# A decoder layer on one core: the output product's results kept in fixed PSUM banks, its operands formed three steps ahead by GpSimd

## The chip, the core and the metric

The kernel runs on one core of a Trainium2 chip. The core has five engines that run side by side, each with its own queue, in order: TensorE (PE in the profile; PEld are its weight loads), VectorE (DVE), ScalarE (ACT), GpSimd (POOL) and SyncE (SP), which here only issues transfers. TensorE writes its products into PSUM, eight banks of 128 x 512 float32; VectorE and ScalarE read and write PSUM and SBUF, GpSimd and transfers SBUF alone. The metric is the device time of one execution in microseconds (us).

## The reference, cut to what matters

One layer, 1024 tokens by 1024 columns, float32. Only the end of it is touched:

```python
y_conv = (u * silu(z_conv)) @ w_conv_out
y_att = (att * silu(z_att)) @ w_att_out
merged = sigmoid(g_conv) * y_conv + sigmoid(g_att) * y_att
x = x + gate * (merged @ w_o)
return x * rsqrt(mean(x * x) + EPS) * final_g
```

## The kernel before

**Split products.** Every float32 operand is split in a high half (a ScalarE copy to a rounded type) and a low half (value minus high half, on VectorE or GpSimd). `mm3` (lines 72 to 75) multiplies high by high (line 73), high by low and low by high, so one 128 x 128 block costs three products. A step of the last stages is 12 products of 128 x 512.

**Steps.** The code calls `at(step, rank, fn)` to put a piece of work at a step. `serve_steps` (line 1064) then goes through the steps and writes the instructions out: first EARLY, then the step's group of products, then COPY, EVICT and HIGH (ScalarE), POOLED (GpSimd), POST_ (mostly VectorE) and LOAD (transfers on SP). Within a step and a rank the order is that of the `at` calls. In these stages the order on every engine, GpSimd too, is the order in which the code is written out. In the attention stage GpSimd's order is left to the scheduler, and the other engines' is written out.

**Merge, steps 0 to 15.** For each of 8 blocks d of 128 columns and each half of the tokens, `merge(d, half)` makes y_att in one bank. Then VectorE multiplies it by the gate `sg[d]` into `sg[d]` (line 1691) and adds that to `merged[d // 4]` (line 1692). The gates are loaded from `ascr` into two buffers in turn, tag `tmp` (line 1677), and pass through a sigmoid on ScalarE (line 1700).

**Output, steps 16 to 43.** The product with w_o is done for the row blocks t = p and t = p + 4 together, in four pairs p, by Strassen's scheme in Winograd's form: 7 block products of 12 in place of 8. The seven left operands ("forms", tile `wf`) are made from four blocks of `merged`, called a11, a12, a21, a22: s1 = a21 + a22, then a21 + a11, then a11 + s1, then s4 = a12 + a11. A form's high half is made on line 1818, its low half on line 1821. In pair 0 VectorE makes most of the sums and low halves (lines 1829 to 1832); in pairs 1 to 3 GpSimd makes all of them. The right operands are blocks of w_o (`woh`, `wol`) and four weight sums (`hh`, `hl`, made by `combo`, lines 1713 to 1716). The partial results are carried on by ScalarE copies from bank to bank and to the tile `xy` (`copy`, line 1855), and TensorE goes on adding to the copies.

**After the product.** `gated` (lines 1766 to 1771) multiplies the result by the gate row into the SBUF tile `s4y`, adds that to the x row tile `xt` and lets ScalarE square `xt` into the bank, summing up the squares. `out_norm` (lines 1777 to 1785) turns the sums into 1 / rms by a short chain with a square root on ScalarE (lines 113 to 118), scales `xt` by it and by final_g (line 1784), and SP stores the two halves.

**Weight sums.** The four sums of blocks of w_o are made by `out_combos(c)` (lines 1519 to 1535, tile `oc`) for two column parts c at the beginning of the attention stage, and stored to `tscr`. The attention stage is counted in slots from -11 on; `in_steps(generator, slots)` runs a generator from yield to yield at these slots. The same SP queue loads the next weights (`wraw`, line 62, split on lines 57 and 58) and moves the k and q tiles (line 1265). Later, `combo` loads the sums again in the merge steps.

The lines that the prediction's steps touch, as the profile numbers them:

Of the kernel before, what the change touches and what calls it, by code (L numbers as in the profile page):

```python
# [39 lines left out]
def layer(ctx: ExitStack, tc: tile.TileContext, a, out):  # L40
# [1478 lines left out]
    def out_combos(c):  # L1519
        t = b11, b12, b22, b21 = [ap_.tile([P, S], F32, name="oc", tag="oc", bufs=4) for _ in range(4)]  # L1520
        for x, n, kp in zip(t, (0, 1, 1, 0), (c, c, 2 + c, 2 + c)):
            nc.sync.dma_start(x, a["w_o"][n, kp])
# [4 lines left out]
        nc.gpsimd.tensor_sub(b21, b21, b22)
# [4 lines left out]
        nc.scalar.activation(b22, b22, AF.Copy, scale=-1.0)
        for x, i in ((b22, 1), (b21, 3)):
            nc.sync.dma_start(tscr[i][c], x)
        yield
# [146 lines left out]
    def merge(d, half):  # L1682
        s = cols_of(half)
        ps = bank()
# [4 lines left out]
        def post():  # L1689
            m = merged[d // 4][:, d % 4, s]  # L1690
            nc.vector.tensor_mul(sg[d][:, s], ps, sg[d][:, s])
            nc.vector.tensor_add(m, m, sg[d][:, s])  # L1692
        at(now[0], POST_, post)

    for d in range(KT):
        for half in (range(2) if d < KT - 1 else (1, 0)):
# [3 lines left out]
        at(2 * d, EVICT, lambda d=d: nc.scalar.activation(sg[d], sg[d], AF.Sigmoid))  # L1700
# [60 lines left out]
    def gated(t, n, c0, c1, ps, first=None):  # L1761
        y = late["sy"][:, 512:512 + c1 - c0]
        g = rows_of["gate_b"][:, c0:c1]
        if first:
            x, op = first
            nc.vector.tensor_tensor(y, x[0], x[1], op=op)
            nc.vector.tensor_mul(y, y, g)
        else:
            nc.vector.tensor_mul(y, ps, g)
        nc.vector.tensor_add(xs[t][:, c0:c1], xs[t][:, c0:c1], y)  # L1770
        nc.scalar.activation(ps, xs[t][:, c0:c1], AF.Square, accum_out=sums_[t][:, n:n + 1])

    def out_norm(t, cuts):
# [24 lines left out]

    def out_pair(p):
        step = OUT + 7 * p  # L1800
        rows = [slice(t * P, t * P + P) for t in (p, p + 4)]
        a11, a12, a21, a22 = (merged[kh][:, :, r] for r in rows for kh in range(2))
        v = (lambda t: t.rearrange("p (k c) -> p k c", k=4))
        s1, box = s1_t, {}
        first_ = p == 0

        def s4():
            return late["sy"][:, 0:512]

        class Form2(Pieces):  # L1810


            def __init__(self, n, src, high_at, low_at, eng):
                def high():
                    tag = ("wlo", "wlo", "whi", "whi", "wraw", "wraw", "wraw")[n]
                    Pieces.__init__(self, wpool.tile([P, 1024], F32R, name="wf", tag=tag,
                                                     bufs=3 if tag == "wraw" else 2))
                    nc.scalar.activation(v(self.hi), src(), AF.Copy)
                at(high_at, HIGH, high)
                at(low_at, POST_ if eng is nc.vector else POOLED,  # L1820
                   lambda: eng.tensor_sub(v(self.lo), src(), v(self.hi).bitcast(F32)))  # L1821

        P_, D_ = nc.gpsimd, nc.vector
        x_at = step - 3 if p else OUT
        for t in (p, p + 4):
            at(x_at, LOAD, lambda t=t: x_load(t))
        if first_:
            f11 = Form2(0, lambda: a11, 12, 12, P_)
            at(step - 1, POST_, lambda: D_.tensor_add(v(s1), a21, a22))
            fs1 = Form2(1, lambda: v(s1), step, step, D_)  # L1830
            at(step, POST_, lambda: D_.tensor_add(a21, a21, a11))
            at(step, POST_, lambda: D_.tensor_add(a11, a11, v(s1)))
            fs2 = Form2(2, lambda: a11, step + 1, step + 1, D_)
            f12 = Form2(3, lambda: a12, step + 1, step + 1, D_)
            at(step + 1, POOLED, lambda: P_.tensor_add(v(s4()), a12, a11))
            fs3 = Form2(4, lambda: a21, step + 2, step + 2, D_)
            fs4 = Form2(5, lambda: v(s4()), step + 3, step + 3, P_)
            f22 = Form2(6, lambda: a22, step + 4, step + 4, P_)
        else:
            at(step - 3, POOLED, lambda: P_.tensor_add(v(s1), a21, a22))  # L1840
            f11 = Form2(0, lambda: a11, step - 3, step - 2, P_)
            at(step - 2, POOLED, lambda: P_.tensor_add(a21, a21, a11))
            at(step - 2, POOLED, lambda: P_.tensor_add(a11, a11, v(s1)))
            fs1 = Form2(1, lambda: v(s1), step - 2, step - 1, P_)
            fs2 = Form2(2, lambda: a11, step - 1, step, P_)
            f12 = Form2(3, lambda: a12, step, step + 1, P_)
            at(step + 1, POOLED, lambda: P_.tensor_add(v(s4()), a12, a11))
            fs3 = Form2(4, lambda: a21, step + 1, step + 2, P_)
            fs4 = Form2(5, lambda: v(s4()), step + 2, step + 3, P_)
            f22 = Form2(6, lambda: a22, step + 3, step + 4, P_)  # L1850
# [7 lines left out]
        def g0():  # L1858
            box["a"] = bank()
            block(box["a"], f11, b_block(0, 0), True)  # L1860

        def g1():
            box["g"] = bank()
            block(box["g"], fs1, combo_block(1), True)
# [103 lines left out]
```

## Time and profile before

| | us |
|---|---|
| median of 3 runs | 1241.06 (1239.45 to 1243.01) |
| the profiled execution's own time | 1237.34 |
| its span, first to last instruction | 1235.5 |
| TensorE busy in that span | 1190.4 (96%) |
| VectorE / ScalarE / GpSimd busy | 943.6 / 608.0 / 538.7 |
| merge steps, from the span's start | 1075.0 to 1118.5 |
| output steps | 1118.5 to 1223.1 |

A row of the timeline has the start from the span's start, the duration, the engine, the line of the code, the operation, the tiles (out<-in), the shapes, a count, and in brackets how long the engine had been idle and who ended that. A row of the waits has who waited for whom, us in total, times, and the longest. Matmuls overlap, so 0.39 us of one stands for a shorter distance from start to start.

### The profile page before, as it was taken

The page shows a single profiled execution, that of the slowest core. Times are in us where ns is not written, and L with a number is a line of the kernel's source. Part 1 is how long each engine was busy: PE and PEld are TensorE (multiplying, and loading weights), DVE is VectorE, ACT ScalarE, POOL GpSimd, SP SyncE. Part 2 cuts the span into 40 slices and gives each one's busy share as a digit, 9 for nine tenths or more (in the row PEclk, how much of TensorE's full clock was granted, in tenths as well). Part 3 has the DMA queues.
Part 4 walks back from the last instruction along what each step waited for, and adds up shares of the span by engine and source line. Part 5 has one row for each costly group of instructions (what it writes and reads, how often), then busy time and mean ns, then how long its engine had stood idle before and what let it go on. Part 6 is the DMA issues. An engine that isn't in the chain of part 4 may idle for free.

```text
span 1235.5 us, 17394 instructions
## 1 busy us (share of the span) xinstructions
PE 1190.4 (96%) x5982; PEld 991.9 (80%) x5982; DVE 943.6 (76%) x1478; ACT 608.0 (49%) x1249; POOL 538.7 (44%) x376
## 2 busy tenths in 40 slices
PE   9999999999999999999989999999999999996995
PEld 7787888888888888788868888888888888884774
DVE  7879999999999998794447667867867733576686
ACT  5655244544544445812037666666656653443432
POOL 0005778788688775743432111111111112175772
PEclk9999999999999999999999999999999999997998
DMA  9584333322423248657896655665665646694221
GB/s 358 187 313 144 117 106 102 119 85 77 129 81 124 86 137 310 252 171 258 190 271 197 142 141 155 171 165 130 182 187 128 178 126 189 240 331 188 63 74 68
DMA packets 103309, 206.01 MB, mean 167 GB/s; under 512 B 29939, under 2 KB 43571, under 8 KB 103222
## 3 DMA queue, kind: packets, MB, share of 16 engines
q1 hardware_dynamic: 86544, 198.30, 51.3%
q10 hardware_dynamic: 16678, 6.61, 1.9%
q8 instruction: 47, 0.77, 0.3%
q14 instruction: 40, 0.33, 0.1%
HBM read 129.59 MB, written 43.82 MB: 140 GB/s over the span
## 4 chain that ended last, share of the span: by engine, by line
PE 76%; DMA 6%; DVE 5%; POOL 4%; issue 4%; ACT 3%; SPq 1%; DVEq 0%; POOLq 0%; ACTq 0%
PE d L75 20%; PE d L73 20%; PE d L74 20%; PE d L604 6%; PE o L1372 4%; PE s L1335 3%; PE t L1351 2%; POOL wf L1821 2%; DMA sgr<-ascr 1%; DVE merged L1692 1%; DMA oc<-in_w_o 1%; DMA ascr<-gs 1%; DMA wraw<-in_w_t 1%; DMA x<-in_xT 1%; DMA tscr<-oc 1%
## 5 line engine op out<-in xcount | busy, mean ns | idle before, releaser
L546 DVE SCALAR_TENSOR_TENSOR acc<-u,cw,acc 128x1024 f32<-128x1024 f32 x232 | 298.8, 1288 | 6.6
L73 PE MATMUL d<-hh,whi 128*128 128x512 f32 x752 | 295.7, 393 | 2.5 <-ACT gs L1024 2.2
L75 PE MATMUL d<-hh,wlo 128*128 128x512 f32 x752 | 293.9, 391 | 2.3 <-POOL wlo L58 2.3
L74 PE MATMUL d<-hl,whi 128*128 128x512 f32 x752 | 293.9, 391 | 0.0
L457 POOL TENSOR_TENSOR wlo<-wraw,whi 128x512 fp32r<-128x512 f32 x130 | 175.4, 1359 | 216.4 <-ACT whi L454 216.2
L58 POOL TENSOR_TENSOR wlo<-wraw,whi 128x512 fp32r<-128x512 f32 (+1 forms) x56 | 82.5, 1490 | 340.1 <-ACT whi L57 326.3
L75 PEld LDWEIGHTS d<-hh,wlo 128*128 128x128 f32 x752 | 141.4, 188 | 32.8 <-POOL wlo L58 2.7
L73 PEld LDWEIGHTS d<-hh,whi 128*128 128x128 f32 x752 | 141.7, 188 | 29.6 <-ACT gs L1024 2.7
L74 PEld LDWEIGHTS d<-hl,whi 128*128 128x128 f32 x752 | 141.7, 188 | 26.1
L454 ACT ACTIVATE whi<-wraw 128x512 fp32r<-128x512 f32 x130 | 79.1, 624 | 86.7 <-DMA wraw<-in_w_co 26.6
L1344 ACT ACTIVATE sb<-sb,stats 128x128 f32<-128x128 f32 (+1 forms) x192 | 84.8, 443 | 31.4 <-DVE stats L1340 31.2
L1340 DVE CUSTOM_DVE_ANT_0 sb<-s,mask 128x128 f32<-128x128 f32 (+1 forms) x192 | 59.7, 348 | 51.1 <-PE s L1335 49.8
L1351 PE MATMUL t<-ident,sb 128*128 128x128 f32 x280 | 74.1, 278 | 4.9 <-DVE pl L1169 4.9
L1372 PE MATMUL o<-ph,vt 128*64 128x128 f32 (+1 forms) x432 | 66.0, 254 | 0.0
L1166 ACT ACTIVATE ph<-t 128x384 fp32r<-128x384 f32 (+2 forms) x96 | 45.6, 475 | 37.8 <-PE t L1351 25.4
L1169 DVE TENSOR_TENSOR pl<-t,ph 128x384 fp32r<-128x384 f32 (+2 forms) x96 | 51.9, 541 | 15.1 <-ACT ph L1166 14.6
L1166 ACT ACTIVATE kqp<-rot 128x512 fp32r<-128x512 f32 x24 | 23.1, 963 | 70.2 <-DVE rot L1189 43.2
L1335 PE MATMUL s<-k,ql 128*128 128x128 f32 (+1 forms) x192 | 55.2, 293 | 0.0
L1372 PE MATMUL o<-pl,vt 128*64 128x128 f32 (+1 forms) x216 | 53.0, 262 | 0.0
L1335 PE MATMUL s<-k,q 128*128 128x128 f32 (+1 forms) x192 | 51.3, 273 | 0.0
L73 PE MATMUL d<-uh,whi 128*128 128x512 f32 x128 | 50.0, 390 | 1.2 <-ACT gs L613 1.2
L604 PE MATMUL d<-whi,hh 128*128 128x512 f32 x128 | 50.5, 394 | 0.0
(348 smaller groups left out, 2798.6 us busy)
## 6 DMA issues: line engine op xcount, KB each, us to landing
wraw<-in_w_t SPq DMA_DIRECT2D x67, 512.0 KB, 4.3
k<-kqp SPq DMA_DIRECT2D x96, 128.0 KB, 2.4
q<-kqp SPq DMA_DIRECT2D x96, 128.0 KB, 2.4
wraw<-in_w_v SPq DMA_DIRECT2D x19, 512.0 KB, 4.6
wa<-in_w_ada SPq DMA_DIRECT2D x16, 512.0 KB, 5.4
ql<-kqp SPq DMA_DIRECT2D x48, 128.0 KB, 2.4
wg<-wscr SPq DMA_DIRECT2D x48, 128.0 KB, 3.0
hscr<-x SPq DMA_DIRECT2D x8, 512.0 KB, 3.1
```

The costliest lines, as they stand in the source:

```text
L58: (lo_eng or nc.vector).tensor_sub(lo, raw, hi.bitcast(F32))
L73: nc.tensor.matmul(ps, lh, rh, start=start, stop=False, skip_group_check=again)
L74: nc.tensor.matmul(ps, lh, rl, start=False, stop=False, skip_group_check=again)
L75: nc.tensor.matmul(ps, ll, rh, start=False, stop=stop, skip_group_check=again)
L454: nc.scalar.activation(self.hi, src(), AF.Copy)
L457: nc.gpsimd.tensor_sub(self.lo, src(), self.hi.bitcast(F32))
L546: nc.vector.scalar_tensor_tensor(acc, u[:, k:k + S], cw[:, ct, k:k + 1], acc, op0=mult, op1=add)
L604: nc.tensor.matmul(ps[i], l[:, k, c], r, start=k == 0 and n == 0, stop=k == KT - 1 and n == 2)
L1335: products.append((w, lambda c=c, w=w, l=x[:, ts_], r=k[:, ks], i=i: nc.tensor.matmul(ps[:, c:c + w], l, r, start=i == 0, stop=i == 1)))
L1344: nc.scalar.activation(sb[:, c:c + w], sb[:, c:c + w], AF.Exp, bias=stats[:, t, h, 1:2], scale=-1.0, accum_out=stats[:, t, h, 0:1])
L1351: yield from ((lambda c=c: nc.tensor.transpose(ps[:, c:c + P], sb[:, c:c + P], ident)) for c in range(0, o, P))
L1372: nc.tensor.matmul(out_, l, r, **kw))
```

## The change

- **Banks.** The pool of eight banks that were handed out in turn becomes eight named banks (`p_bank`). A merge step uses bank step % 8; pair p uses four fixed ones, 0 to 3 or 4 to 7.
- **Results stay in PSUM.** Merge multiplies into the bank and adds from it to `merged`. `gated` works in the bank throughout (gate, then residual), the squares read the bank and are written to SBUF, and `out_norm` takes the bank as its input. `xt` is only read until then.
- **Forms.** Every form's high half is put three steps ahead of its product and its low half two, all low halves and sums on GpSimd, for all four pairs. The first form of pair 1 gets step 17, ahead of the other six of pair 0.
- **Order.** The last four merge groups become (6, 1), (7, 1), (6, 0), (7, 0), and the sigmoid of d = 7 moves one step ahead. The loads of the weight sums and of the last blocks of w_o move ahead.
- **Weight sums.** All four subtractions and additions are GpSimd's, one per slot, each stored in the slot of the next. The negation of one of them moves from there into `combo`, on ScalarE.

```diff
 def out_combos(c):
-        nc.gpsimd.tensor_sub(b11, b11, b12)
-        yield
-        nc.vector.tensor_sub(b12, b12, b22)
-        nc.gpsimd.tensor_add(b22, b22, b11)
-        nc.gpsimd.tensor_sub(b21, b21, b22)
-        yield
-        for x, i in ((b11, 0), (b12, 2)):
-            nc.sync.dma_start(tscr[i][c], x)
-        yield
-        nc.scalar.activation(b22, b22, AF.Copy, scale=-1.0)
-        for x, i in ((b22, 1), (b21, 3)):
-            nc.sync.dma_start(tscr[i][c], x)
+        yield
+        steps = ((nc.gpsimd.tensor_sub, b11, b11, b12), (nc.gpsimd.tensor_sub, b12, b12, b22),
+                 (nc.gpsimd.tensor_add, b22, b22, b11), (nc.gpsimd.tensor_sub, b21, b21, b22))
+        for i, (op, *args) in enumerate(steps):
+            if i:
+                store()
+            op(*args)
+            store = lambda x=args[0], i=(0, 2, 1, 3)[i]: nc.sync.dma_start(tscr[i][c], x)
+            yield
+        store()
         yield
...
-    in_steps(out_combos(0), [-11, -8, -4, -2])
-    in_steps(out_combos(1), [-1, 2, 4, 6])
+    in_steps(out_combos(0), [-11, -8, -7, -6, -5, -3])
+    in_steps(out_combos(1), [-2, 1, 2, 3, 4, 6])
...
+    def p_bank(i):
+        return pd.tile([P, 512], F32, name="d", tag=f"d{i % 8}")
...
 def merge(d, half):
-            nc.vector.tensor_mul(sg[d][:, s], ps, sg[d][:, s])
-            nc.vector.tensor_add(m, m, sg[d][:, s])
+            nc.vector.tensor_mul(ps, ps, sg[d][:, s])
+            nc.vector.tensor_add(m, ps, m)
...
-        at(2 * d, EVICT, lambda d=d: nc.scalar.activation(sg[d], sg[d], AF.Sigmoid))
+        at(2 * d - d // 7, EVICT, lambda d=d: nc.scalar.activation(sg[d], sg[d], AF.Sigmoid))
...
-    for step, i, c, tag in ((0, 1, 0, "wlo"), (1, 1, 1, "wlo"), (3, 2, 0, "wraw"), (5, 2, 1, "wraw"), (7, 3, 0, "wlo"),
-                            (9, 3, 1, "wlo"), (11, 4, 0, "wraw"), (12, 4, 1, "wraw")):
+    for step, i, c, tag in ((0, 1, 0, "wlo"), (1, 1, 1, "wlo"), (2, 2, 0, "wraw"), (4, 2, 1, "wraw"), (5, 3, 0, "wlo"),
+                            (7, 3, 1, "wlo"), (8, 4, 0, "wraw"), (10, 4, 1, "wraw")):
         combo(step, i, c, tag)
...
-        late_b(13 + 2 * c, c)
+        late_b(12 + 2 * c, c)
...
 def gated(t, n, c0, c1, ps, first=None):
...
-            nc.vector.tensor_mul(y, ps, g)
-        nc.vector.tensor_add(xs[t][:, c0:c1], xs[t][:, c0:c1], y)
-        nc.scalar.activation(ps, xs[t][:, c0:c1], AF.Square, accum_out=sums_[t][:, n:n + 1])
+            nc.vector.tensor_tensor(ps, first[0], first[1], op=first[2])
+        nc.vector.tensor_mul(ps, ps, rows_of["gate_b"][:, c0:c1])
+        nc.vector.tensor_add(ps, ps, xs[t][:, c0:c1])
+        nc.scalar.activation(late["sy"][:, 512:512 + c1 - c0], ps, AF.Square, accum_out=sums_[t][:, n:n + 1])
...
 def out_norm(t, cuts, halves):
...
-            nc.vector.scalar_tensor_tensor(xs[t][:, s], xs[t][:, s], r, rows_of["fg_b"][:, s], op0=mult, op1=mult)
+            nc.vector.scalar_tensor_tensor(xs[t][:, s], halves[n], r, rows_of["fg_b"][:, s], op0=mult, op1=mult)
...
+    slots_of = [[OUT] + [OUT + 2 + i for i in range(6)], [OUT + 1] + [OUT + 8 + i for i in range(6)],
+                [OUT + 14 + i for i in range(7)], [OUT + 21 + i for i in range(7)]]
+    class Block(Pieces):
+        def __init__(self, step, src):
+            def high():
+                tag = TILES[(step - OUT) % 7]
+                Pieces.__init__(self, wpool.tile([P, 1024], F32R, name="wf", tag=tag, bufs=3 if tag == "wraw" else 2))
+                nc.scalar.activation(v4(self.hi), src(), AF.Copy)
+            at(step - 3, HIGH, high)
+            at(step - 2, POOLED, lambda: nc.gpsimd.tensor_sub(v4(self.lo), src(), v4(self.hi).bitcast(F32)))
...
 def out_pair(p):
+        n11, ns1, ns2, n12, ns3, ns4, n22 = slots_of[p]
+        at(ns1 - 4, POOLED, lambda: plus(v4(s1_t), a21, a22))
+        f11 = Block(n11, lambda: a11)
+        at(ns1 - 3, POOLED, lambda: plus(a21, a21, a11))
+        at(ns1 - 3, POOLED, lambda: plus(a11, a11, v4(s1_t)))
+        fs1 = Block(ns1, lambda: v4(s1_t))
+        fs2 = Block(ns2, lambda: a11)
+        f12 = Block(n12, lambda: a12)
+        at(ns4 - 4, POOLED, lambda: plus(s4(), a12, a11))
+        fs3, fs4, f22 = Block(ns3, lambda: a21), Block(ns4, s4), Block(n22, lambda: a22)
+        at(n12, POST_, lambda: gated(t1, 0, 0, 512, box["a"]))
+        at(ns3 + 1, POST_, lambda: gated(t2, 1, 512, 1024, box["g"], (box["y"], box["g"], sub)))
+        at(ns4 + (not end), POST_, lambda: gated(t1, 1, 512, 1024, box["b"], (box["b"], box["x"], add)))
+        at(ns4 + 1, POST_, lambda: out_norm(t1, 2, (box["a"], box["b"])))
+        at(n22, POST_, whole)
+        at(n22 + (not end), POST_, lambda: out_norm(t2, 3 if end else 2, (box["d"], box["g"])))
```

The names in the prediction: a form's "own" step is n11, ns1 and so on; "late weights" are the two blocks that `late_b` loads, split at steps 16 and 17 ahead of the forms of the same step; "slot" is the attention stage's count.

More of the change, by code (lines that the diff above doesn't have):

```diff
@@ L1683, in merge @@
         s = cols_of(half)
-        ps = bank()
+        ps = p_bank(now[0])
         for k in range(4):
@@ L1761, in gated, with out_norm @@
     def gated(t, n, c0, c1, ps, first=None):
[L1762 to L1763 removed]
         if first:
[L1765 to L1768, printed above, removed]
[L1769 to L1773 removed]
+            nc.vector.tensor_tensor(ps, first[0], first[1], op=first[2])
+        nc.vector.tensor_mul(ps, ps, rows_of["gate_b"][:, c0:c1])
+        nc.vector.tensor_add(ps, ps, xs[t][:, c0:c1])
+        nc.scalar.activation(late["sy"][:, 512:512 + c1 - c0], ps, AF.Square, accum_out=sums_[t][:, n:n + 1])
+    def out_norm(t, cuts, halves):
         ss = sums_[t]
@@ L1797, in combo_block @@
         return rhs
-    def out_pair(p):
[L1800 to L1805, printed above, removed]
-        def s4():
[L1808 to L1850, printed above, removed]
@@ new lines, in layer, with v4, high @@
+    slots_of = [[OUT] + [OUT + 2 + i for i in range(6)], [OUT + 1] + [OUT + 8 + i for i in range(6)],
+                [OUT + 14 + i for i in range(7)], [OUT + 21 + i for i in range(7)]]
+    TILES = ("wlo", "wraw", "wlo", "whi", "whi", "wraw", "wraw")
+    by_step = {}
+    def v4(t):
+        return t.rearrange("p (k c) -> p k c", k=4)
+    class Block(Pieces):
+        def __init__(self, step, src):
+            def high():
+                tag = TILES[(step - OUT) % 7]
[3 more added lines that the diff above has]
+            at(step - 2, POOLED, lambda: nc.gpsimd.tensor_sub(v4(self.lo), src(), v4(self.hi).bitcast(F32)))
@@ new lines, in out_pair @@
+    def out_pair(p):
+        n11, ns1, ns2, n12, ns3, ns4, n22 = slots_of[p]
+        t1, t2, end = p, p + 4, p == 3
+        a11, a12, a21, a22 = (merged[kh][:, :, t * P:t * P + P] for t in (t1, t2) for kh in range(2))
+        box, plus = {}, nc.gpsimd.tensor_add
+        banks = {x: 4 * (p % 2) + i for i, x in enumerate("abgd")}
+        def s4():
+            return v4(late["sy"][:, 0:512])
+        for t in (t1, t2):
+            at(n11 - 3 if p > 1 else OUT + 4 * p, LOAD, lambda t=t: x_load(t))
+        at(ns1 - 4, POOLED, lambda: plus(v4(s1_t), a21, a22))
[7 more added lines that the diff above has]
+        fs3, fs4, f22 = Block(ns3, lambda: a21), Block(ns4, s4), Block(n22, lambda: a22)
@@ L1852, in copy @@
         def copy(key, src, scale=1.0, sbuf=None):
             def fn():
-                box[key] = bank() if sbuf is None else late["xy"][:, cols_of(sbuf)]
+                box[key] = p_bank(banks[key]) if sbuf is None else late["xy"][:, cols_of(sbuf)]
                 nc.scalar.activation(box[key], box[src], AF.Copy, scale=scale)
             return fn
[L1858 to L1864, printed above, removed]
@@ L1866, in more, with begin, fn @@
-        def more(key, form, rhs):
-            return lambda: block(box[key], form, rhs, False, True)
+        def begin(key, form, rhs):
+            def fn():
+                box[key] = p_bank(banks[key])
+                block(box[key], form, rhs, True)
+            by_step[now_of[key]] = fn
+        def more(step, key, form, rhs):
+            by_step[step] = lambda: block(box[key], form, rhs, False, True)
         def last():
@@ L1892, in whole @@
                 gated(t2, 0, 0, 512, box["d"])
-        at(step + 6, POST_, whole)
-        at(step + 6 + (not end), POST_, lambda: out_norm(t2, 3 if end else 2))
-        groups.extend([g0, g1, more("b", fs2, combo_block(2)), more("a", f12, b_block(0, 1)),
-                       more("d", fs3, combo_block(3)), more("b", fs4, b_block(1, 1)),
-                       last if end else more("d", f22, combo_block(4))])
+        at(n22, POST_, whole)
+        at(n22 + (not end), POST_, lambda: out_norm(t2, 3 if end else 2, (box["d"], box["g"])))
     for p in range(4):
         out_pair(p)
+    groups += [by_step[x] for x in sorted(by_step)]
     serve_steps(groups)
```

35 lines of the change are left out of this document (21 added, 14 removed).

## The prediction

> **What bounds the kernel now.** I read the page's busy shares first, then the last stage in stretches.
>
> ```profile
> PE 1190.4 (96%) x5982; PEld 991.9 (80%) x5982; DVE 943.6 (76%) x1478; ACT 608.0 (49%) x1249; POOL 538.7 (44%) x376
> ```
>
> TensorE (PE) is the bound over the whole, so a change off TensorE pays only where TensorE stops. These stretches cover the merge groups (steps 0 to 15), the four output pairs and the tail; after the length come each engine's busy time, then the granted clock and the DMA share.
>
> ```profile
> 1075.00:1118.50 43.50, 43.50 (x193) 36.06 (x192) 29.76 (x28) 19.81 (x24) 28.83 (x14) 1.00 0.92 338
> 1118.50:1152.84 34.34, 23.96 (x85) 18.04 (x84) 21.51 (x17) 12.31 (x20) 17.54 (x10) 0.80 0.26 101
> 1152.84:1176.19 23.35, 21.21 (x86) 16.75 (x84) 17.36 (x30) 10.58 (x24) 19.49 (x14) 0.93 0.29 91
> 1176.19:1198.97 22.78, 21.26 (x85) 16.67 (x84) 18.42 (x28) 8.66 (x20) 17.64 (x12) 0.93 0.27 93
> 1198.97:1223.12 24.15, 21.85 (x97) 17.25 (x95) 18.11 (x31) 8.75 (x22) 11.84 (x8) 0.93 0.12 44
> 1223.12:1235.50 12.38, 0.00 (x0) 0.00 (x0) 6.72 (x23) 1.70 (x8) 0.00 (x0) 0.67 0.23 85
> ```
>
> The merge groups never stop: 43.5 us for 16 steps of 12 products, 2.72 us a step or 0.227 a product, so step k starts at 1075.0 + 2.72k. The 28 output steps would take 28 x 2.72 = 76.2 us at that rate; the four rows sum to 104.6. **28.4 us are lost**: 15.3 in the first pair (34.34 - 7 x 2.72), 4.3, 3.7 and 5.1 in the others. The matrix clock is part of it: 0.93 over 23.35 us is 1.6 us. What TensorE waits for in that stage:
>
> ```profile
> PE d L75 <- DVE wf L1821: 5.5, 2, 4.1
> PE d L73 <- ACT wf L1818: 4.9, 2, 2.7
> PE d L75 <- POOL wf L1821: 3.4, 3, 2.1
> PE d L73 <- ACT d L1855: 2.5, 3, 1.3
> ```
>
> Three of the four are the forms (wf): their high halves from ScalarE (ACT), their low halves from VectorE (DVE) or GpSimd (POOL). The first pair's come late by a chain that the timeline shows:
>
> ```profile
> 1112.34 0.32 SPq L1677 DMA_DIRECT2D sgr<-ascr  x1
> 1118.08 1.06 ACT L1700 ACTIVATE sgr<-sgr 128x1024 f32<-128x1024 f32 x1 [3.49 <-DMA sgr<-ascr]
> 1120.62 2.74 DVE L1829 TENSOR_TENSOR s<-merged,merged 128x512 f32<-128x512 f32 x1
> 1126.04 2.82 DVE L1821 TENSOR_TENSOR wf<-s,wf 128x512 fp32r<-128x512 f32 x1
> 1128.92 0.79 PE L75 MATMUL d<-hh,wf 128*128 128x512 f32 x1 [4.05 <-DVE wf L1821]
> 1158.61 0.50 PE L75 MATMUL d<-hh,wf 128*128 128x512 f32 x1 [2.05 <-POOL wf L1821]
> ```
>
> The last gate (sg 7) is issued at 1112.34, when VectorE has let go of its buffer, and lands by 1118.08; the sum s1 and the low half behind it take 2.74 and 2.82 us. In the other pairs ScalarE's queue stands behind the squares, which wait for VectorE, and the high halves behind them come late:
>
> ```profile
> ACT d L1771 <- DVE xt L1770: 25.8, 12, 3.3
> ```
>
> **The prices.** From the tile views (min/median/max in ns), a group, and two rows side by side:
>
> ```profile
> L1691 DVE TENSOR_TENSOR sgr<-d,sgr x16: 676/681/692, 1078.6 to 1123.3; 128x512 f32<-128x512 f32 x16
> L1692 DVE TENSOR_TENSOR merged<-merged,sgr x16: 692/1384/2181, 1079.4 to 1124.0; 128x512 f32<-128x512 f32 x16
> ...
> DMA to landing us min/median/max: 3.6/4.5/7.0
> ```
>
> ```profile
> L1821 POOL TENSOR_TENSOR wf<-merged,wf x17: 1277/1733/1820, 1116.8 to 1215.0; 128x512 fp32r<-128x512 f32 x17
> L1734 POOL TENSOR_TENSOR oh<-wt,oh x2: 2355/2571/2787, 1125.5 to 1134.5; 128x1024 fp32r<-128x1024 f32 x2
> L1818 ACT ACTIVATE wf<-merged 128x512 fp32r<-128x512 f32 x20 | 12.2, 621 | 6.4 <-POOL merged L1843 6.4
> 1171.18 1.29 POOL L1840 TENSOR_TENSOR s<-merged,merged 128x512 f32<-128x512 f32 x1
> 1171.58 0.69 DVE L1766 TENSOR_TENSOR s4y<-xy,d 128x512 f32<-128x512 f32 x1 [1.51 <-ACT xy L1855]
> ```
>
> A VectorE operation with one input in PSUM takes 0.68 every time (L1691, 676 to 692). With both inputs in SBUF (L1692) it takes up to 2.18 while GpSimd works, and GpSimd's own then takes 1.73 in place of 1.28. The last two rows overlap, one input of L1766 is in PSUM, and both run at their short price. The change leaves VectorE no 512-column operation with two SBUF inputs in this stage, so I take 0.69 for VectorE and 1.28 (512 columns) and 2.36 (1024) for GpSimd, with 1.73 and 2.79 as the other end. A VectorE result written to PSUM is in no row: from below 0.68, from above the 2.18 of the slowest; I take 0.69, nearest to L1691, which differs only in where it writes. At 1.4, VectorE's ten operations per pair would be 14 us, and with out_norm's some 5 fill the 19.04 of a pair: some 8 us of the gain would go, tail included.
>
> **The change, part by part.**
>
> *Merge.* The second operation reads PSUM and SBUF: 0.69 for a median of 1.38. TensorE is busy all 43.5 us, so that saves nothing there; but sg is now let go by the first operation of each half. Its last reader before sg 7's load is half (5,1), whose products end with step 11 at 1107.6; 0.69 later, at 1108.4, the load goes out, 3.9 us sooner than in the row. Landing: 3.6 to 7.0; I take 5.0, between the median and the 5.7 of this same transfer: 1113.4. The order (7,1) before (6,0) puts what s1 needs at step 13. The negation on ScalarE now stands here, twice 1.06 us; ScalarE is busy 19.8 of 43.5 and the last is at step 7, so it costs nothing; uncovered it would be 2.1.
>
> The weight sums' loads move up to three steps forward in SP's queue, past gate and merged loads: at 338 GB/s one load of 0.524 MB, 1.55 us, now lies ahead of sg 7 that lay behind it, and I count it within the 5.0. Their low halves and those of w_ao fill 28.8 of GpSimd's 43.5, so only the last, behind sg 7, is late.
>
> *First pair.* ScalarE: sigmoid 1.06 to 1114.5, the last weight sum's high half to 1115.5. GpSimd, in its order: that sum's low half 2.36 to 1117.9, s1 to 1119.2, the first form's low half to 1120.5. TensorE wants that at its third product, 1119.0: **a stop of 1.5**. The step ends at 1120.5 + 10 x 0.227 = 1122.8. GpSimd goes on with two sums and the other early form, 3 x 1.28, to 1124.3 (due at 1123.3); then come the two late weights, each 2.36, *ahead* of the two forms that are due. Their high halves stand behind the bank copy after each step (0.6 + 1.06), so the first is ready at 1124.5: low half to 1126.8, fs1 to 1128.1 (due at 1127.0), second late weight to 1130.5, fs2 to 1131.8 (due at 1130.8). So step 19 ends at about 1134.1; unhindered it would be 1075.0 + 20 x 2.72 = 1129.4. Loss 4.7. With the clock halved after the stops, each as 1.6 above, up to 8. I take 6.6 in place of 15.3.
>
> *Other pairs.* GpSimd has 11 operations per pair: 14.1 us of 19.04 (at 1.73: 19.0, just full). A form's low half is asked for two steps before its product; the tightest is fs1, behind the first form, two sums and its own: 4 x 1.28 + 1.1 for ScalarE's copy and high half = 6.2 us after a mark that lies 8.2 + 0.45 before the product, so 2.4 to spare. (At 1.73: 0.6.) Loss 0 in place of 13.1. The squares read PSUM and write SBUF; what waits behind them on ScalarE is now wanted three steps later. The fixed banks come free a pair before they are asked for. The x loads keep their steps (16, 20, 27, 34) and their place between the out stores.
>
> *Tail.* From the last y copy the chain is VectorE's, with the same number of operations and GpSimd at rest, so 12.38 stays.
>
> *Weight sums.* These stand at the start of the attention stage, and the trace shows TensorE stopping right there:
>
> ```profile
> 618.90:655.84 36.94, 30.29 (x144) 25.07 (x144) 19.65 (x44) 15.56 (x37) 14.32 (x9) 0.95 0.88 271
> ```
>
> ```profile
> 617.58 2.37 POOL L1527 TENSOR_TENSOR oc<-oc 128x1024 f32<-128x1024 f32 x1
> 621.21 0.50 PE L75 MATMUL d<-hh,wlo 128*128 128x512 f32 x1 [2.26 <-POOL wlo L58]
> 631.30 0.80 SPq L1534 DMA_DIRECT2D tscr<-oc  x2
> 638.05 0.90 SPq L62 DMA_DIRECT2D wraw<-in_w_t  x2
> 645.77 0.63 ACT L57 ACTIVATE whi<-wraw 128x512 fp32r<-128x512 f32 x1 [5.21 <-DMA wraw<-in_w_t]
> 649.76 0.30 PE L1351 MATMUL t<-ident,sb 128*128 128x128 f32 x1 [4.09 <-DVE pl L1169]
> ```
>
> Idle 36.94 - 30.29 = 6.65, and 0.05 of the clock is 1.8: 8.5 us. The later 6.2: SP stores the last sums at 631.30, behind ScalarE's negation, the next sums' loads wait for those stores, and the weights queue behind them until 638.05; ScalarE then stands at them until 645.77. Without the negation the last store is a slot earlier, SP reaches the sums' loads at about 630 and the weights at about 631.7: 6 us sooner, landing near 642, in time for 645.45. From 0 to 6.2; I take 5. The first stop (2.26) is a weight's low half behind a sum of 2.37 on GpSimd. One sum moves there from VectorE and the others are emitted later; GpSimd's order here is the scheduler's, so -2.4 (one more ahead) to 2.3 (none); I take 0. SP now waits at each store for one sum; k and q moves queue behind it.
>
> **Sum:** 28.4 - 6.6 = 21.8, and 5: 26.8 us. Span 1235.5 to 1208.7; the profiled execution's 1237.3 to 1210.5; the runs shown have a median 3.7 above that execution, so 1241.1 - 26.8 = **1214**.
>
> [...]
>
> **Rivals.** *The gate still lands late* (0.2). DMA is 92% busy in the merge stretch at 338 GB/s, 1.55 us per load of 0.524 MB, and one more weight sum is loaded ahead of sg 7. Landing at 1118.1 as before, the whole chain shifts by 4.7: first pair 9.4 to 12.7, and if the weight sums then bring nothing either: 1241 - 17 = 1224. Against: the load goes out earlier.
>
> *GpSimd becomes the bound* (0.08). At 1.73 and 2.79 its 44 operations of 512 columns and 3 of 1024, from 1115.5, end at 1115.5 + 76.1 + 8.4 = 1200.0, and the last step after that at 1203 to 1205, where the forecast has 1194.7 + 6.6 = 1201.3: with nothing from the sums, 1222. [...]
>
> *All stops go* (0.10): 28.4 + 8.5 = 36.9, or 1204.
>
> *Slower: SP held by the sums* (0.05). Eight stores now each wait for a GpSimd sum (2.37) that may stand behind two low halves (2 x 1.28): 40 us if nothing covers them, with weights and k/q moves queued behind, which the 649.76 row shows ending in a TensorE stop. It decides from 22 us uncovered; at 28, 1247. Against: a slot of some 3 us lies between one store and the next.
>
> *Nothing moves* (0.03): the waits on the forms only change their releaser.
>
> **Numbers.** Forecast 0.54 (1207 to 1219). Below 0.3%, some 4 us, a measurement of this kernel can't tell from none. Faster 0.92, same 0.03, slower 0.05. The range from all forms in time to a late gate: 1204 to 1227.
>
> **What would show it.** Merge's second operation at 0.69, GpSimd's 512-column ones near 1.28; sg 7 issued near 1108; one or two short stops in steps 16 to 19, none later with clock 1.00; the wait at L1771 gone; weights issued near 632 and no stop at 645. Wrong would be: stops in pairs 1 to 3, VectorE over 0.8 on PSUM results, or a longer stretch from 600 to 660.

## The result and the profile after

The changed kernel takes 1230.7 us, median of 7 runs (1226.6 to 1235.3), against 1240.1 for the kernel before on the same chip (median of 7): a ratio of 0.9921, 95% interval 0.9894 to 0.9949. It is faster, by 9.4 us where 26.8 were forecast; 1230.7 lies above the range of 1204 to 1227. The profiled execution has a span of 1224.8 (own time 1226.6), 10.7 less than before.

The stretches of the changed kernel, cut at the starts of steps 0, 16 and 20 and at TensorE's last product. Columns: the stretch, its length, busy time and instructions of PE, PEld, DVE, ACT and POOL, granted clock, DMA share, GB/s.

```profile
1072.75:1116.27 43.52, 43.52 (x193) 35.94 (x192) 19.16 (x29) 24.78 (x29) 26.11 (x15) 1.00 0.93 359
1116.27:1135.66 19.39, 13.42 (x49) 9.97 (x49) 2.45 (x4) 6.26 (x10) 17.72 (x13) 0.91 0.37 135
1135.66:1212.66 77.00, 69.38 (x301) 56.03 (x299) 51.62 (x92) 30.99 (x72) 44.13 (x36) 0.96 0.20 69
1212.66:1224.80 12.14, 0.00 (x1) 0.00 (x0) 6.74 (x23) 1.48 (x8) 0.00 (x0) 0.69 0.23 86
```

The merge steps still never stop. The 28 output steps take 96.4 us in place of 104.6. At 2.72 a step, steps 16 to 19 lose 8.5 us (19.39 - 10.88) and steps 20 to 43 lose 11.7 (77.00 - 65.28). Before, cut in the same way, these were 15.3 and 13.2. So the first part gained 6.8 and the rest only 1.5, where nearly all 13 were to go. The tail gained 0.2, and the merge stage begins 2.25 us earlier: together 10.7.

The prices were right. The tile views of the changed kernel give min/median/max in ns:

```profile
L1692 DVE TENSOR_TENSOR d<-d,sgr x16: 689/700/700, 1076.4 to 1117.4; 128x512 f32<-128x512 f32 x16
```

```profile
L1693 DVE TENSOR_TENSOR merged<-d,merged x16: 691/692/693, 1077.1 to 1118.1; 128x512 f32<-128x512 f32 x16
```

```profile
L1817 POOL TENSOR_TENSOR wf<-merged,wf x20: 1265/1288/1298, 1119.3 to 1204.2; 128x512 fp32r<-128x512 f32 x20
```

A VectorE result in PSUM (L1692) costs 0.70, and GpSimd's low halves are at 1.29 throughout (before: 1.73). Cheap operations did not empty the queues. What TensorE waits for in the output steps, and ScalarE's longest wait there:

```profile
ACT s4y L1772 <- DVE d L1771: 31.5, 12, 5.1
...
PE d L73 <- ACT d L1844: 6.3, 2, 4.0
PE d L75 <- POOL wf L1817: 6.0, 3, 3.7
...
PE d L73 <- ACT xy L1844: 1.3, 1, 1.3
```

The forms (L1817) stop TensorE in steps 16 to 19 only. The wait for copies from bank to bank (L1844), 2.5 us before (L1855), is now 6.3, and 1.3 more for a copy to `xy`. ScalarE's wait for VectorE ahead of the squares did not go; it grew from 25.8 (L1771 before) to 31.5.

**The late copies, steps 20 to 43.** The timeline of the changed kernel at the turn from pair 1 to pair 2:

```profile
1165.52 0.70 DVE L1771 TENSOR_TENSOR d<-d,xt 128x512 f32<-128x512 f32 x1
1167.74 1.24 DVE L1778 TENSOR_TENSOR r<-ss 128x1 f32<-128x1 f32 x1 [1.52 <-ACT s4y L1772]
...
1170.41 1.41 DVE L1785 SCALAR_TENSOR_TENSOR xt<-d,r,fg_b 128x512 f32<-128x512 f32 x2
1171.73 0.69 DVE L1770 TENSOR_TENSOR d<-d,gate_b 128x512 f32<-128x512 f32 x1
1172.46 0.70 DVE L1771 TENSOR_TENSOR d<-d,xt 128x512 f32<-128x512 f32 x1
```

```profile
1173.25 0.60 ACT L1772 ACTIVATE s4y<-d 128x512 f32<-128x512 f32 x1 [3.85 <-DVE d L1771]
...
1173.84 0.59 ACT L1844 ACTIVATE d<-d 128x512 f32<-128x512 f32 x1
```

```profile
1174.48 0.80 PE L73 MATMUL d<-hh,wf 128*128 128x512 f32 x1 [4.01 <-ACT d L1844]
```

VectorE waits 1.52 us for ScalarE's square sums and then goes through the whole norm of row block t1 (1167.74 to 1171.7) before it touches the last result, d, of row block t2, whose products had ended with step 29 at 1164.9. The square of d on ScalarE waits 3.85 us for that, and behind the square stands the next pair's copy, which TensorE needs at once. The same happens one pair later (a stop of 2.29), and smaller at 1162.01 (1.27). Of the 11.7 us lost in steps 20 to 43, these three stops are 7.6 and the slower clock behind the longest (0.50 from 1172.97 to 1179.79) is 2.6.

**The first pair, steps 16 to 19.** The issues between 1106 and 1115 (KB, us to landing), then the chain:

```profile
sgr<-ascr SPq DMA_DIRECT2D x1, 512.0 KB, 6.8
```

```profile
1106.71 0.32 SPq L1678 DMA_DIRECT2D sgr<-ascr  x1
```

```profile
1113.61 1.06 ACT L1701 ACTIVATE sgr<-sgr 128x1024 f32<-128x1024 f32 x1 [5.18 <-DMA sgr<-ascr]
```

```profile
1115.75 2.38 POOL L1722 TENSOR_TENSOR hl<-wt,hh 128x1024 fp32r<-128x1024 f32 x1 [4.76 <-ACT hh L1720]
1118.09 1.26 POOL L1831 TENSOR_TENSOR s<-merged,merged 128x512 f32<-128x512 f32 x1
1119.31 1.26 POOL L1817 TENSOR_TENSOR wf<-merged,wf 128x512 fp32r<-128x512 f32 x1
```

```profile
1120.63 0.50 PE L75 MATMUL d<-oh,wf 128*128 128x512 f32 x1 [3.71 <-POOL wf L1817]
...
1129.66 0.50 PE L75 MATMUL d<-hh,wf 128*128 128x512 f32 x1 [1.69 <-POOL wf L1817]
```

This is the forecast chain link by link, only later against the products.

**The weight sums.** In the attention stage of the changed kernel:

```profile
609.90 10.44 POOL L1529 TENSOR_TENSOR oc<-oc 128x1024 f32<-128x1024 f32 x4 [0.92 <-DMA oc<-in_w_o]
620.30 4.92 POOL L58 TENSOR_TENSOR wlo<-wraw,whi 128x512 fp32r<-128x512 f32 x4
```

```profile
622.81 0.50 PE L75 MATMUL d<-hh,wlo 128*128 128x512 f32 x1 [3.82 <-POOL wlo L58]
...
646.37 0.93 PE L1351 MATMUL t<-ident,sb 128*128 128x128 f32 x4 [1.29 <-ACT sb L1344]
```

GpSimd makes the four sums in a row. The first stop grew from 2.26 to 3.82, the second shrank from 4.09 to 1.29.

### The profile page after: what moved, and what is told of

Same layout as the page of the kernel before. It is cut to its first block, busy times and chain, and to the rows that moved or that the text cites. A ratio compares the mean times of both kernels' runs of the same rounds, so it can differ in the third digit from the quotient of the medians.

```text
span 1224.8 us, 17371 instructions
## 1 busy us (share of the span) xinstructions
PE 1185.0 (97%) x5982; PEld 988.6 (81%) x5982; DVE 911.1 (74%) x1469; ACT 608.4 (50%) x1249; POOL 538.2 (44%) x385
## 4 chain that ended last, share of the span: by engine, by line
PE 81%; DVE 6%; ACT 4%; POOL 3%; DMA 2%; issue 2%; SPq 0%; DVEq 0%; ACTq 0%; POOLq 0%
PE d L73 21%; PE d L75 21%; PE d L74 21%; PE d L604 6%; PE o L1372 4%; PE s L1335 3%; PE t L1351 3%; PE d L275 1%; ACT hh L239 1%; DVE hl L242 1%; DVE xt L1785 1%; POOL wf L1817 1%; DMA raws<-in_w_ao 1%; DVE wa L170 1%; DMA sgr<-ascr 1%
## 5 line engine op out<-in xcount | busy, mean ns | idle before, releaser
L73 PE MATMUL d<-hh,whi 128*128 128x512 f32 x752 | 295.6, 393 | 2.2 <-ACT gs L1024 2.2
L73 PEld LDWEIGHTS d<-hh,whi 128*128 128x128 f32 x752 | 141.8, 189 | 29.2 <-ACT gs L1024 2.7
L73 PE MATMUL d<-uh,whi 128*128 128x512 f32 x128 | 49.9, 390 | 1.2 <-ACT gs L613 1.2
```

The lines of the kernel that those rows point to most:

```text
L73: nc.tensor.matmul(ps, lh, rh, start=start, stop=False, skip_group_check=again)
```

## The experiments

All lengths below come from the profile of one execution each, worked out as above: "13 to 19" and "20 to 43" are the us lost there against 2.72 a step. The column "output steps" is the time of steps 16 to 43 with what steps 13 to 15 lost added to it; that was 0.9 us in e3, 0.7 in e4, 1.2 in e5, 3.6 in e6, 0.3 in e9, 5.0 in e11, and nothing in the others. "Ahead" is the time from the last `uh` product of the stage before (596.39 in the changed kernel) to the first merge product (1072.75): it holds all that the weight sums can do. The expectations of e5 and e9 count from the start of the first stop, 22.6 us later in the changed kernel (453.8 there is 476.4 here). The ratio is against the kernel before, run on the same chip, over several runs. The two products between which "ahead" is counted, in the changed kernel:

```profile
596.39 0.39 PE L75 MATMUL d<-uh,wlo 128*128 128x512 f32 x1
```

```profile
1072.75 0.39 PE L73 MATMUL d<-ah,whi 128*128 128x512 f32 x1
```

| kernel | ahead | 13 to 19 | 20 to 43 | output steps | ratio (95%) |
|---|---|---|---|---|---|
| before | 478.6 | 15.3 | 13.2 | 104.6 | 1 |
| changed | 476.4 | 8.5 | 11.7 | 96.4 | 0.9921 (0.9894 to 0.9949) |
| e1, norm of t1 later | 476.8 | 8.6 | 1.7 | 86.5 | 0.9848 (0.9808 to 0.9888) |
| e2, first forms earlier | 480.7 | 7.2 | 12.3 | 95.7 | 0.9938 (0.9917 to 0.9960) |
| e3, late weights later | 476.6 | 6.6 | 15.5 | 98.3 | 0.9960 (0.9926 to 0.9994) |
| e4, old weight sums | 478.3 | 10.2 | 12.0 | 98.4 | 0.9955 (0.9933 to 0.9977) |
| e5, sums' slots later | 474.7 | 10.7 | 11.8 | 98.7 | 0.9944 (0.9917 to 0.9971) |
| e6, results in SBUF | 476.5 | 14.2 | 21.2 | 111.6 | 1.0047 (1.0023 to 1.0071) |
| e7 = e1 + e2 + e3 | 476.7 | 1.5 | 2.8 | 80.5 | 0.9838 (0.9796 to 0.9880) |
| e8 = e7 + e5 | 475.4 | 2.6 | 2.8 | 81.6 | 0.9833 (0.9789 to 0.9877) |
| e9, sums on VectorE | 475.5 | 9.8 | 13.1 | 99.1 | 0.9919 (0.9891 to 0.9948) |
| e10 = e7 + e9 | 471.8 | 1.7 | 2.8 | 80.6 | 0.9780 (0.9748 to 0.9812) |
| e11 = e1 + e6 | 480.1 | 15.6 | 15.5 | 107.3 | 0.9991 (0.9968 to 1.0015) |

**e1: the norm of t1 one step later.**

```diff
-        at(ns4 + 1, POST_, lambda: out_norm(t1, 2, (box["a"], box["b"])))
+        at(n22 + (not end), POST_, lambda: out_norm(t1, 2, (box["a"], box["b"])))
```

> One change to the changed kernel: in pairs 0 to 2 the row norm of the first row group (t1) is emitted one step later, behind the last gated piece (d) of the second row group. Theory A (order of queues): in the changed kernel VectorE works through the whole norm of t1, which waits twice for ScalarE, before it makes d; so the square of d starts only at 1173.25 and 1197.37 (waits of 3.85 and 3.84 us) and the next pair's bank copies behind it on ScalarE (1173.84, 1197.95) hold TensorE for 4.01 and 2.29 us. Then these two stops and the ones of 1.27 (1162.01) and 0.5 (1155.45) go, steps 20 to 43 lose 1 to 3 us in place of 11.4, and the span is 8 to 10 us shorter than the changed kernel's 1224.8: 1215 to 1217. Rival B (the forms are late by themselves, the copies only end last): the stops stay at the same steps with a form as what ends them, gain under 3 us. Rival C (VectorE is slowed by GpSimd, small operations of 1.0 to 1.25 us): the norm now falls on other steps, gain of 0 to 4 us, and the wait of ScalarE for d stays above 3 us.

Measured: span 1217.1, 7.7 less than the changed kernel's; the output steps are 9.9 shorter (its merge stage began 2.2 later: its last `uh` product already stood at 598.24, in code that is the same). Steps 20 to 43 lose 1.7. Their stretch, and all waits of TensorE in the output steps:

```profile
1137.94:1204.97 67.03, 66.36 (x301) 54.39 (x299) 46.44 (x92) 31.31 (x72) 44.28 (x36) 1.00 0.23 79
```

```profile
PE d L75 <- POOL wf L1817: 5.9, 3, 3.7
PE d L73 <- ACT d L1844: 0.7, 1, 0.7
```

```profile
1168.11 0.60 ACT L1772 ACTIVATE s4y<-d 128x512 f32<-128x512 f32 x1
...
1169.07 0.58 ACT L1844 ACTIVATE d<-d 128x512 f32<-128x512 f32 x1 [0.27 <-PE d L75]
```

The square of d waits no longer, and the copy now waits for TensorE and not TensorE for it. Theory A holds. Rivals B and C fall for these steps: the forms follow the same steps as in the changed kernel and no longer stop TensorE there, and VectorE's small operations of 1.0 to 1.25 us are still in this trace. The kernel before had the same order as e1: its line was `at(step + 5 + 2 * (not end), POST_, lambda: out_norm(t1, 2))`, one step behind `whole`, which makes d. Its rows at the same turn show d (L1769, L1770) ahead of the norm (L1777):

```profile
1178.22 0.69 DVE L1769 TENSOR_TENSOR s4y<-d,gate_b 128x512 f32<-128x512 f32 x1
1178.95 0.87 DVE L1770 TENSOR_TENSOR xt<-xt,s4y 128x512 f32<-128x512 f32 x1
1179.74 1.24 DVE L1777 TENSOR_TENSOR r<-ss 128x1 f32<-128x1 f32 x1
```

The change moved t1's norm a step forward, ahead of d, and that move alone costs the 10 us.

**e2: the first forms of pairs 0 and 1 at step 12.**

```diff
-            at(step - 3, HIGH, high)
-            at(step - 2, POOLED, lambda: nc.gpsimd.tensor_sub(v4(
+            at(early or step - 3, HIGH, high)
+            at(early or step - 2, POOLED, lambda: nc.gpsimd.tensor_sub(v4(
...
-        f11 = Block(n11, lambda: a11)
+        f11 = Block(n11, lambda: a11, 12 if p < 2 else None)
```

> One change to the changed kernel: the first forms of pairs 0 and 1 (a11, high and low) are made at step 12, where GpSimd stands idle for 4.76 us, in place of steps 13 to 15. Theory A: the stop of 3.71 us in step 16 comes from that form's low half, which stands behind the last weight sum's low half and the sum s1 on GpSimd; with it the clock loses 1.4 us. Then step 16 takes about 2.8 in place of 7.86 us and the span is about 4 to 5 us shorter. Rival: GpSimd stays the limit of the first pair whatever the order (two late weights of 2.4 us and the sums stand ahead of the forms of steps 18 and 19); the stop moves to steps 18 and 19, steps 16 to 19 lose 5 to 7 us in place of 8.5, and the gain is 1.5 to 3.5 us.

```profile
1134.24 0.80 PE L75 MATMUL d<-hh,wf 128*128 128x512 f32 x1 [4.35 <-POOL wf L1817]
```

Steps 16 and 17 take 2.72 each, but step 18 takes 9.39: its form stops TensorE for 4.35 us. The stop moved and the gain is 1.3 of 8.5, close to what the rival said. "Ahead" is 480.7 here, 4.3 more than in the changed kernel, in code that is the same there. Of that, 3.4 is the granted clock: it is 0.50 for 10.2 us of the stretch in e2 (624.30 to 631.13, 658.43 to 661.84) and for 3.4 us in the changed kernel (623.42 to 626.83). Why e2's stops there fell out otherwise stays open.

**e3: the late weight blocks behind the forms.**

```diff
-        at(OUT + c, HIGH, high)
-        at(OUT + c, POOLED, lambda: nc.gpsimd.tensor_sub(wol
+        at(OUT + 1 + 3 * c, HIGH, high)
+        at(OUT + 1 + 3 * c, POST_, lambda: nc.gpsimd.tensor_sub(wol
```

> One change to the changed kernel: the halves of the last two weight blocks (1,2) and (1,3), first used in step 22, are made at steps 17 and 20 behind the forms, not at 16 and 17 ahead of them. Theory A: the stops of 1.69 and 0.58 us in steps 18 and 19 come from forms standing behind these blocks' low halves (2.4 us each) on GpSimd; steps 18 and 19 then take 2.8 each in place of 4.70 and 3.60, a gain of 2 to 3 us. Rival: the sums for fs1 and fs2 come late from step 16 on whatever stands between; gain under 1 us, and the stop stays where it is or moves to step 22 with the weight as what ends it.

Steps 18 and 19 take 2.72 each in place of 4.70 and 3.60: A's cause is right. But small stops come up in steps 22, 24 and 26 (0.24, 0.52, 1.47), the first of them on the moved weight, as the rival had it. By the table's column the output steps are 1.9 longer: 0.9 is lost in step 15, where a high half stops TensorE for 0.72, and 1.6 is clock lost in steps 39 and 40 (below). Alone it gains nothing.

**e7: the three together.** (In the expectation 95.2 stands for 95.7.)

> The three single edits on the output steps together: norm of t1 one step later, first forms at step 12, last two weight blocks at steps 17 and 20. Alone they changed the output steps (16 to 43) from 96.4 us to 86.5, 95.2 and 98.3. Theory A (two causes in the first pair, each covering the other: the first form stands behind the last weight sum, and the second and third stand behind the two late weight blocks): together steps 16 to 19 lose 0 to 2 us in place of 8.5, steps 20 to 43 lose 1 to 4, and the output steps take 78 to 82 us; span about 1209. Rival (GpSimd is simply full in the first pair: what is taken from steps 16 to 19 comes back in steps 20 to 27): the output steps take 84 to 88 us, span about 1216.

```profile
1116.40:1128.82 12.42, 11.18 (x50) 8.93 (x48) 2.65 (x5) 4.85 (x8) 12.26 (x9) 1.00 0.55 212
1128.82:1196.85 68.03, 66.86 (x301) 54.24 (x299) 46.37 (x92) 32.26 (x73) 47.50 (x37) 1.00 0.23 78
```

Theory A: steps 16 to 19 lose 1.5 us, the rest 2.8, the clock is 1.00 in both. In the first pair two causes covered each other: mended alone, e2 gains 1.3 us and e3 1.9 in steps 13 to 19, mended together 7.0. The execution traced is the fastest of e7's four; in the medians the gain over e1 is smaller than in the traces (1216.3 and 1218.2) and the intervals overlap.

**e6 and e11: what the PSUM results are worth.** Both put the results of merge, gate, residual and norm back into SBUF.

```diff
-            nc.vector.tensor_mul(ps, ps, sg[d][:, s])
-            nc.vector.tensor_add(m, ps, m)
+            nc.vector.tensor_mul(sg[d][:, s], ps, sg[d][:, s])
+            nc.vector.tensor_add(m, m, sg[d][:, s])
...
-        nc.vector.tensor_mul(ps, ps, rows_of["gate_b"][:, c0:c1])
-        nc.vector.tensor_add(ps, ps, xs[t][:, c0:c1])
-        nc.scalar.activation(late["sy"][:, 512:512 + c1 - c0], ps, AF.Square, accum_out=sums_[t][:, n:n + 1])
+            nc.vector.tensor_mul(y, ps, g)
+        nc.vector.tensor_add(xs[t][:, c0:c1], xs[t][:, c0:c1], y)
+        nc.scalar.activation(ps, xs[t][:, c0:c1], AF.Square, accum_out=sums_[t][:, n:n + 1])
```

> One change to the changed kernel: the results go back to SBUF. Merge's product and sum, the gated pieces, the residual and the norm read and write SBUF as in the kernel before; order, steps and GpSimd's forms are the changed kernel's. Theory A (the PSUM results are what lets GpSimd alone make the forms): VectorE's operations take 1.0 to 2.2 us again and GpSimd's 1.7 in place of 1.28; GpSimd's 11 operations per pair then take 18.7 of the 19.04 us, steps 20 to 43 lose 18 us or more in place of 11.4, and the span is 7 to 14 us longer than 1224.8. Rival B (the order of the queues decides, the price of an operation hardly): steps 20 to 43 lose 10 to 14 us, at the same steps, and the span is within 3 us of 1224.8.

> Two edits to the changed kernel: results back in SBUF (which alone took the output steps from 96.4 to 111.6 us) and the norm of t1 one step later (which alone took them to 86.5). What is the PSUM placing worth once the order is mended? Theory A (the placing pays by itself, because VectorE's and GpSimd's operations block each other in SBUF): steps 20 to 43 still lose 8 us or more where the mended order with PSUM results lost 1.4, and steps 15 to 19 lose about 14; output steps 97 to 103 us. Rival (the slow operations only showed because d stood last on VectorE): steps 20 to 43 lose 1 to 4 us, output steps 90 to 94 us.

Two tile views of e6:

```profile
L1693 DVE TENSOR_TENSOR merged<-merged,sgr x16: 691/1682/2192, 1078.5 to 1124.6; 128x512 f32<-128x512 f32 x16
```

```profile
L1821 POOL TENSOR_TENSOR wf<-s,wf x4: 1267/1738/1744, 1135.4 to 1203.5; 128x512 fp32r<-128x512 f32 x4
```

The operations take their long prices again, and e6 is slower than the kernel before; its span is 16.8 us longer than the changed kernel's, more than the 7 to 14 expected. In the order of e1 the placing is worth 20.8 us of steps 13 to 43 (107.3 against 86.5), 7.0 in steps 13 to 19 and 13.8 after. So theory A both times; e11's 107.3 lies above its 97 to 103, and 102.3 of it are steps 16 to 43. e11 takes as long as the kernel before (ratio 0.9991): of what e1 gains over before, all comes with the PSUM placing, and forms from GpSimd three steps ahead bring nothing measurable without it. What the placing brings with the old forms was not run.

**e4, e5, e8, e9 and e10: the weight sums.** e4 takes that part of the change back, as the diff of the change shows it. e5 moves the slots; e9 leaves them and changes the engine:

```diff
-    in_steps(out_combos(0), [-11, -8, -7, -6, -5, -3])
-    in_steps(out_combos(1), [-2, 1, 2, 3, 4, 6])
+    in_steps(out_combos(0), [-8, -5, -4, -3, -2, -1])
+    in_steps(out_combos(1), [0, 3, 4, 5, 6, 7])
```

```diff
-        steps = ((nc.gpsimd.tensor_sub, b11, b11, b12), (nc.gpsimd.tensor_sub, b12, b12, b22),
-                 (nc.gpsimd.tensor_add, b22, b22, b11), (nc.gpsimd.tensor_sub, b21, b21, b22))
+        steps = ((nc.vector.tensor_sub, b11, b11, b12), (nc.vector.tensor_sub, b12, b12, b22),
+                 (nc.vector.tensor_add, b22, b22, b11), (nc.vector.tensor_sub, b21, b21, b22))
```

> One change to the changed kernel: the part on the weight sums alone is taken back (one of the four sums on VectorE, negation on ScalarE in the attention stage, the old slots). The last stage is the changed one. Theory A: that part brought what the first product of the merge stage shows, 1075.0 to 1072.75: with it undone that product starts at 1075.0, the span is 2 to 2.5 us longer, the stop at 645 is 4.1 us again and the one at 621 about 2.3. Rival: the 2.25 us came from elsewhere (other transfers in the attention stage); the first merge product stays at 1072 to 1073.

> One change to the changed kernel: the slots of the weight sums in the attention stage are moved two to three slots later (first set -8 to -1, second set 0 to 7). Measured from the start of the stop at 619 to the first merge product, the changed kernel takes 453.8 us, the kernel before 456.0. Theory A: the stop of 3.82 us at 622.8 is a weight's low half that stands behind four sums in a row on GpSimd (10.44 us); with the sums later that stop falls to 2.3 or less and the stretch to 450 to 452 us. Rival: the sums' loads and stores then stand on SP's queue ahead of other weights and another stop takes its place; the stretch stays at 453 to 456 us, or gets longer, up to 458.

> One change to the changed kernel: the four weight sums of each set run on VectorE, where one took 1.21 us, in place of GpSimd (10.4 to 11.2 us for four in a row); slots, loads and stores stay. Theory A: the stop of 3.1 to 3.8 us at 622 to 625 is a weight's low half behind four sums in a row on GpSimd; moving their slots changed nothing, since GpSimd's order stays (sums first). Then that stop falls to 0 to 1.5 us and the stretch from its start to the first merge product goes from 453.8 to 449 to 452 us. Rival: the low half waits for its load or for the memsets ahead of it and not for the sums: the stop stays at 2 to 4 us. Rival 2: VectorE is the engine that sets the order there (scaling of the attention inputs), a stop of 2 to 5 us moves to it and the stretch takes 454 to 458 us.

With the old sums "ahead" is 478.6 and 478.3 in two traces (e4's merge stage begins at 1078.5, but its last `uh` product stood 3.8 us later already). e4's first stop is 2.32 as expected, its second 2.35 and not 4.1. With the changed kernel's own code up to there "ahead" is 476.4 to 476.8 in five (the changed kernel, e1, e3, e6, e7) and 480.1 and 480.7 in two (e11, e2). So with that part the stretch is 1.5 to 2.3 us shorter in five traces of seven and longer in two, and the ratios of e4 and of the changed kernel overlap: what it is worth is not settled. e5's own trace is about where its theory A had it (a stop of 1.10, a stretch of 452.1), but by its ratio it is no faster than the changed kernel, and e8, with the same slots, has a stop of 3.81: GpSimd still makes four sums in a row, and where that row begins differs by some us from run to run (at 606.63 in e5; behind a transfer at 612.30 in e8 and at 609.90 in the changed kernel). e9 bears out its theory A for the first stop, which is gone; its stretch of 452.9 lies between theory A and rival 2, and the second stop comes back:

```profile
647.89 0.30 PE L1351 MATMUL t<-ident,sb 128*128 128x128 f32 x1 [2.36 <-DVE pl L1169]
```

So VectorE is the next one there (rival 2's stop, not its length), and the time doesn't change measurably.

> The same three edits with the weight sums' slots two to three later as well. If the edits add, it is faster than the three by what the later sums bring alone (2 to 4 us if the stop at 622 falls, nothing if another stop takes its place): span about 1206 to 1209.

> The three edits on the output steps (norm of t1 one step later, first forms at step 12, last two weight blocks at steps 17 and 20) with the weight sums on VectorE. If the last edit brings 2 to 4 us: span 1205 to 1207, median some 1212 to 1214 in place of 1216.3. If it brings nothing: as the three alone, span 1209 to 1212.

e8 is as fast as e7; its span of 1211.6 lies above the 1206 to 1209 that it was to have if the edits add. e10 is the fastest kernel of the study: 1212.6 us, median of 6, against 1239.6 before, ratio 0.9780 (0.9748 to 0.9812), and it beats the changed kernel as well. Its span of 1206.8 is the one expected if the sums on VectorE bring something. But its lead over e7 lies within the two intervals, and its "ahead" is 471.8 against e9's 475.5 with the same code there: 3.4 of that is the clock, 0.50 from 649.41 to 656.24 in e9 and 1.00 throughout in e10. What the sums on VectorE bring is not settled.

## Why the prediction was wrong

**Prices.** Right: 0.70 for VectorE's PSUM results against 0.69, 1.29 for GpSimd against 1.28. e6 and e11 show that these prices are what the output steps' gain rests on.

**Other pairs: "Loss 0 in place of 13.1".** This is the step that failed: 11.7 us were lost, of the 16.1 by which the trace's gain of 10.7 falls short of 26.8. It rested on "The squares read PSUM and write SBUF; what waits behind them on ScalarE is now wanted three steps later", and on GpSimd's 2.4 us to spare. The second held: no form stopped TensorE after step 19. The first is true of the forms and not of the bank copies, which stand in the same queue and are wanted in the next step. A row quoted in the prediction had already shown TensorE waiting for them (`PE d L73 <- ACT d L1855`, 2.5 us in three stops). And the tail end of each pair was not costed at all: the norm of t1 moved one step forward on VectorE, ahead of d, with its 4 us and two waits for ScalarE. e1 undoes that one line, and the steps lose 1.7 in place of 11.7.

**First pair: 6.6 forecast, 8.5 lost.** The mechanism was right and one term off. Against the first merge product, sg 7 was issued at 33.96 us (forecast 33.4) and ScalarE began on it at 40.86 (forecast 38.4): the landing took 6.8 in place of 5.0, with the DMA engines 92% busy from 1106 to 1115. All that follows comes 2.3 to 2.5 us later than forecast, s1 at 45.34 in place of 42.9, and the stop in step 16 is 3.71 in place of 1.5. Of the 8.5 the three stops are 6.0 (3.71, 1.69, 0.58); the other 2.5 is mostly clock, 0.91 over 19.4 us, which is 1.7. It was 0.50 from 1121.77 to 1125.18, behind the stop of 3.71, and 1.00 behind the other two; in the kernel before it was 0.50 from 1159.12 to 1162.53, behind the stop of 2.05 in the prediction's row of 1158.61.

**Weight sums: 5 forecast, 2.25 gained** (not settled, as said above). The mechanism of the later stop was right: the weights went out at 633.23 (forecast about 631.7, before 638.05), and that stop went from 4.09 to 1.29, with the clock of 0.50 that stood behind it before (650.53 to 653.94, 1.7 us lost) gone as well, some 4.5 of the up to 6.2. The first stop was put at 0 inside bounds of -2.4 to 2.3. It went from 2.26 to 3.82, and the slow clock now stands behind it (623.42 to 626.83, 1.7 us lost): some -3.3. The rest of the 2.25 is mostly a stop of 0.79 at 992.13 that the changed kernel does not have. With GpSimd's order left to the scheduler, four sums in a row was past the bad end of that range.

**Tail: "12.38 stays".** 12.14.

**The rivals.** A gate that lands late came true in part, by 2.4 of its 4.7 us. GpSimd as the bound did not: it is idle 33 of the 77 us after step 19. "All stops go" is nearly what e10 does in the output steps with three more edits there (80.6 against 76.2).

## What to carry to other kernels

When an operation gets cheaper, read the order of each in-order queue anew: here 10 us hung on one norm standing ahead of a result that another engine's queue, and behind it TensorE, was waiting for. Of everything that stands behind a wait, cost the one that is wanted soonest, not the class that was moved to safety. Where two causes cover each other, an edit of one alone shows nothing; test them together before dropping either.
